# Stick-breaking attention taken by pairs of heads, sums and top-k steps paced, gates multiplied into the output weights of two half projections

## The chip, the cores and the metric

The kernel runs on one core of one Trainium2 chip. The core has TensorE (PE, with its weight loads listed as PEld), VectorE (DVE), ScalarE (ACT), GpSimd (POOL) and SyncE (SP, which only issues transfers). The metric is the device time of one execution in microseconds; lower is better.

## The reference

Two layers, each a mixer and a SwiGLU block, over 512 tokens of width 1024 in float32. Six vectors a layer, made from `c` by one product with `w_mod`, shift, scale and gate them. The change touches the first half of layer 0, the even mixer, and the output projection of layer 1's mixer.

```python
mod = einsum('bd,ldm->lbm', silu(c), w_mod) + b_mod       # per layer: sh_m, sc_m, g_m, sh_f, sc_f, g_f
h = x * (1 + sc_m) + sh_m
# layer 0: even mixer
z = q_sb @ k_sb.T * 64**-0.5                               # 8 heads, 512 x 512
log_keep = where(past, log_sigmoid(-z), 0)
suffix = reverse_cumsum(log_keep) - log_keep
o_sb = where(past, exp(log_sigmoid(z) + suffix), 0) @ v_sb
score = sum_h relu(q_ix @ k_ix.T * 64**-0.5)[h] * w_ix[h]  # 4 index heads; the best 128 keys of each row are kept
o_dsa = softmax(masked(rope(q_dsa) @ rope(k_dsa).T)) @ v_dsa   # 8 heads
y = concat(o_sb, o_dsa) @ w_out_even
# layer 1: differential attention, then y = o @ w_out_odd
x = layer_norm(ALPHA * x + (1 + g_m) * y)
x = layer_norm(ALPHA * x + (1 + g_f) * swiglu(x * (1 + sc_f) + sh_f))
```

## The kernel before

Everything is laid out by a Python program that issues instructions for tiles; a scheduler then puts them in a fixed order on each engine (earlier in the program comes first, but an instruction that is not ready lets later ones past), and allots tile buffers. Generators `yield` the PE time in microseconds that they have just issued, and `weave(main, fill, ratio)` runs `ratio` microseconds of `fill` for each microsecond that `main` yields.

Every float32 operand of a dense product is split into a high part (`wh`, `hh`, `o_h`, float32r, copied by ACT) and a low part (`wl`, `hl`, `o_l`, the difference); `mm3` (L319) makes three products of them and counts as 0.65. `split_w` (L292) splits 128x1024 of weights: ACT copies, and the engine at the head of the list `low` subtracts (`low_on`, L288, sets that list; in layer 0 it is VectorE).

Layer 0's mixer, in program order:
- `proj_tokens` (L987) makes `v_sb`, with `index_scores` (L755) and then `top_keys` (L779) stepped beside it. `top_keys` is 16 rounds of `max` and `match_replace` for each of three blocks of 512, 384 and 256 columns, all on VectorE, one `yield` a round.
- `sb_heads` (L816) is stick-breaking attention. For one head, `scores_of` makes 1280 columns of scores in three PSUM banks (of six in the tag `z`) from float32 operands of 64 rows, each followed by a 128-row product that adds the mask; ACT runs Abs, Exp and Ln, VectorE joins them (L834) and copies the high part `hi` (L835), POOL makes `lo` (L836). `suffix` adds the running sums as 20 products of 128 rows (L847) and ACT takes Exp. `mix` (L855) weighs the values for two heads, one in each half of the columns. Head h+2's scores are issued between the suffixes of two heads.
- `weave(..., rest, SB_FILL)` lays `even_rest` behind it: ten dense 128-column tiles of 24 products each, three pairs of q and k tiles for the later heads and four q tiles with rope for the next part. One step of `topk` goes with each dense step, and one step of `mods0` with each fourth dense step and with each yield of `sb_heads`.
- `mods0` is three calls of `mod_side` (L188). Each loads 16 pieces of `w_mod` (256 KB, tag `wm`, three buffers that also hold the sum `macc`) and adds them up on VectorE, one piece a step (L210, L212); call 2 ends in the gate row `rows[0, 2]` (`grow`), calls 3 and 4 in the shift and scale for the block behind.
- `dsa_heads` (L915) is the sparse attention, a pipeline of 16 units, with `down_beside` (L577) woven in: the first half of the output projection, 32 steps of `mm3`, each finished PSUM bank going through `partial` (L476), which multiplies by `grow` and adds to the residual `xa`. `mods0` is stepped with every second of them, and drained behind.
- `down_last` (L608) is the second half of the projection, followed by layer norm and the transposes `turn` for the SwiGLU block.

Layer 1 does the same with `diff_heads` and `down_beside(w_out_odd[0], ...)` (L1169).

Of the kernel before, what the change touches and what calls it, by code (L numbers as in the profile page):

```python
# [26 lines left out]
SB_FILL = 1.0  # L27
DSA_FILL = 0.65
# [19 lines left out]
def hybrid_kernel(ctx, tc, x, c, positions, w_mod, b_mod, w_in_even, w_out_even, w_in_odd,  # L48
# [139 lines left out]
    def mod_side(l, i, wide=False):  # L188
# [12 lines left out]
        for h in range(2):  # L201
# [12 lines left out]
            if wide:  # L214
                yield
# [260 lines left out]
    def partial(o, b, cs, grow, first):  # L476

        t = wd("yt")[:, :cs.stop - cs.start]
# [300 lines left out]
    def top_keys():  # L779

        for i in range(3, 0, -1):
            sc = scores[i]
            for r in range(16):
# [3 lines left out]
                yield  # L787
# [28 lines left out]
    def sb_heads(qk):  # L816
        Z, WT = {}, {}

        def scores_of(h):
            q, k = qk[h // 2]  # L820
            need(q, k)
            pb = 64 * (h % 2)
            z = Z[h] = [bank("za"), bank("zb"), bank("zc")]
            for s, (i, f, _, n) in enumerate(STRIP):
                pe.matmul(z[i][:, f:f + n], lhsT=k[pb:pb + 64, P * s:P * s + P], rhs=q[pb:pb + 64, P * s:S],
                          start=(f == 0), stop=False, skip_group_check=True)
                pe.matmul(z[i][:, f:f + P], lhsT=ident_r, rhs=bias_sb_r, start=False, stop=True, skip_group_check=True)
            hi, lo = ab("hi", F32R), ab("lo", F32R)
            for i, a, b in SPAN:
                zi, e, l = z[i][:, :b - a], slice(a, b), wd("l")[:, :b - a]  # L830
                act.activation(l, zi, AF.Abs)
                act.activation(l, l, AF.Exp, scale=-1.0)
                act.activation(l, l, AF.Ln, bias=1.0)
                dve.scalar_tensor_tensor(l, zi, 0.0, l, op0=OP.max, op1=OP.add)  # L834
                dve.tensor_copy(hi[:, e], l)  # L835
                pool.tensor_tensor(lo[:, e], l, hi[:, e], op=OP.subtract)  # L836
            WT[h] = hi, lo
            return 4.3 if h > 5 else 2.3

        def suffix(h):  # L840
            z, (hi, lo) = Z[h], WT[h]
            for s in (0, 1, 3, 2):
                i, f, _, n = STRIP[s]
                for s2 in range(s, 4):
                    _, _, c2, n2 = STRIP[s2]
                    for op in (hi, lo):
                        pe.matmul(z[i][:, f + n - n2:f + n], lhsT=negtri_r if s2 == s else negones_r,  # L847
                                  rhs=op[:, c2:c2 + n2], start=False, stop=True, skip_group_check=True)
            w = ab("w")
            for i, a, b in SPAN:  # L850
                act.activation(w[:, a:b], z[i][:, :b - a], AF.Exp)
            WT[h] = w
            return 2.1

        def mix(hp):  # L855
            o = Z[2 * hp + 1][0]
            for s, (_, _, c0, n) in enumerate(STRIP):
                for j in range(2):
                    h = 2 * hp + j
                    pe.matmul(o[64 * j:64 * j + 64, S - n:S], lhsT=v_sb[s][:, 64 * h:64 * h + 64], rhs=WT[h][:, c0:c0 + n],  # L860
                              start=(s == 0), stop=(s == 3), skip_group_check=True)
            put_o(hp, o)
            return 2.1

        yield scores_of(0)
# [416 lines left out]
```

## Time and profile before

| | |
|---|---|
| median of three runs | 1331.32 us (1330.69 to 1336.52) |
| profiled execution, its own time | 1333.38 us |
| its span, first to last instruction | 1331.3 us |
| mean granted TensorE clock | 0.985 of full speed |
| busy: PE, DVE, ACT, POOL | 96%, 67%, 37%, 19% of the span |

The shares are averages over stages with different limits. A busy PE is not a PE at its peak, since the ends of matmuls are modelled: at full rate, matmuls of 512 columns start 0.22 us apart and are each shown as 0.39 us long. So PE's work is counted here from start to start. Stick-breaking attention runs from 95 to 228 us of the span, the sparse attention from 228 to 298, the end of the projection and the layer norm to about 314.

### The profile page before, as it was taken

How to read it: one execution, taken by the hardware profiler on the slowest of the kernel's cores; microseconds unless marked ns; L12 is line 12 of the kernel's file. 1: busy time of each engine (PE TensorE's matmuls, PEld its weight loads, DVE VectorE, ACT ScalarE, POOL GpSimd, SP SyncE). 2: the span in 40 equal slices, each digit the busy share in tenths (PEclk: the TensorE clock that was granted, in tenths of full speed). 3: DMA queues.
4: the chain of work that ended last, by engine and by line, in shares of the span. 5: the costliest groups of instructions: out<-in, count | busy, mean ns of one | idle time of the engine just before them, and what ended most of it. 6: DMA issues, size and time to landing. Idle time of an engine off the chain costs nothing.

```text
span 1331.3 us, 17597 instructions
## 1 busy us (share of the span) xinstructions
PE 1283.0 (96%) x6707; PEld 1017.8 (76%) x6707; DVE 885.8 (67%) x1605; ACT 498.8 (37%) x889; POOL 246.4 (19%) x173
## 2 busy tenths in 40 slices
PE   6999998999999999999999999898999999999995
PEld 5767676668888888888888866676888888888884
DVE  3789996987866665665694387787786335335358
ACT  2445544554432222222244356565443322322210
POOL 0103223001800000000017244443280000000004
PEclk9999989999999999999999999999999999999998
DMA  9953234342365555555423422215235223233211
GB/s 265 279 174 95 88 112 139 99 126 96 92 219 157 192 169 173 190 172 189 141 68 111 127 64 84 88 52 175 78 97 190 75 100 110 95 96 95 95 64 63
DMA packets 134388, 169.47 MB, mean 127 GB/s; under 512 B 7800, under 2 KB 89120, under 8 KB 134304
## 3 DMA queue, kind: packets, MB, share of 16 engines
q1 hardware_dynamic: 133568, 167.31, 39.9%
q8 instruction: 52, 0.85, 0.3%
q10 hardware_dynamic: 576, 1.02, 0.2%
q14 instruction: 32, 0.26, 0.1%
q0 software_dynamic: 160, 0.03, 0.0%
HBM read 159.95 MB, written 2.10 MB: 122 GB/s over the span
## 4 chain that ended last, share of the span: by engine, by line
PE 49%; issue 26%; DVE 13%; ACT 4%; DMA 3%; POOL 3%; SPq 1%; DVEq 0%; ACTq 0%; POOLq 0%
PE po L321 7%; PE po L322 7%; PE po L323 7%; PE pd L321 4%; PE pd L323 4%; PE pd L322 4%; DMA wm<-in_w_mod_dram 2%; PE pv L321 1%; PE pv L322 1%; PE pv L323 1%; DMA rt<-rq 1%; PE pf L322 1%; PE pf L323 1%; PE pf L321 1%; DVE yt L479 1%
## 5 line engine op out<-in xcount | busy, mean ns | idle before, releaser
L295 ACT ACTIVATE wh<-raw 128x1024 fp32r<-128x1024 f32 x174 | 183.8, 1065 | 499.8 <-PE po L322 268.6
L299 DVE TENSOR_TENSOR wl<-raw,wh 128x1024 fp32r<-128x1024 f32 x169 | 238.3, 1414 | 169.5 <-ACT wh L295 169.3
L321 PE MATMUL po<-hh,wh 128*128 128x512 f32 x848 | 340.9, 402 | 0.4 <-DVE sg L631 0.3
L323 PE MATMUL po<-hh,wl 128*128 128x512 f32 x848 | 333.4, 393 | 0.0
L322 PE MATMUL po<-hl,wh 128*128 128x512 f32 x848 | 333.3, 393 | 0.0
L321 PEld LDWEIGHTS po<-hh,wh 128*128 128x128 f32 x848 | 160.6, 189 | 40.0 <-issue 6.4
L323 PEld LDWEIGHTS po<-hh,wl 128*128 128x128 f32 x848 | 160.8, 190 | 34.1
L322 PEld LDWEIGHTS po<-hl,wh 128*128 128x128 f32 x848 | 160.9, 190 | 30.4
L502 POOL TENSOR_TENSOR lnv<-lnv,mhalf 128x1 f32<-128x1 f32 x16 | 11.6, 723 | 683.7 <-DVE lnv L500 683.5
L322 PE MATMUL pd<-wl,hid_h 128*128 128x512 f32 x352 | 137.2, 390 | 0.0
L323 PE MATMUL pd<-wh,hid_l 128*128 128x512 f32 x352 | 137.0, 389 | 0.0
L321 PE MATMUL pd<-wh,hid_h 128*128 128x512 f32 x352 | 137.0, 390 | 0.0
L212 DVE SCALAR_TENSOR_TENSOR macc<-wm,silu_c,macc 128x512 f32<-128x512 f32 x140 | 108.1, 775 | 6.8 <-DMA wm<-in_w_mod_dram 4.6
L631 DVE TENSOR_TENSOR sg<-sg,po 128x512 f32<-128x512 f32 x40 | 27.5, 686 | 118.3 <-PE po L323 118.3
L321 PEld LDWEIGHTS pd<-wh,hid_h 128*128 128x128 f32 x352 | 66.1, 188 | 14.1 <-issue 0.4
L322 PEld LDWEIGHTS pd<-wl,hid_h 128*128 128x128 f32 x352 | 66.1, 188 | 13.8 <-DVE wl L299 0.3
L323 PEld LDWEIGHTS pd<-wh,hid_l 128*128 128x128 f32 x352 | 66.1, 188 | 13.7
L479 DVE TENSOR_TENSOR yt<-pd,grow 128x512 f32<-128x512 f32 x96 | 64.1, 682 | 10.2 <-PE pd L323 10.1
L321 PE MATMUL pd<-wh,o_h 128*128 128x512 f32 x128 | 57.0, 445 | 0.0
L323 PE MATMUL pd<-wh,o_l 128*128 128x512 f32 x128 | 51.8, 405 | 0.0
L322 PE MATMUL pd<-wl,o_h 128*128 128x512 f32 x128 | 51.4, 401 | 0.3 <-DVE wl L299 0.3
L1094 ACT ACTIVATE e<-e,nm 128x128 f32<-128x128 f32 (+3 forms) x64 | 35.4, 555 | 36.8 <-DVE nm L1093 25.2
(276 smaller groups left out, 2021.4 us busy)
## 6 DMA issues: line engine op xcount, KB each, us to landing
wm<-in_w_mod_dram SPq DMA_DIRECT2D x56, 512.0 KB, 5.0
raw<-in_w_gate_dram SPq DMA_DIRECT2D x22, 1024.0 KB, 5.4
raw<-in_w_up_dram SPq DMA_DIRECT2D x22, 1024.0 KB, 5.4
wm<-in_w_mod_dram SPq DMA_DIRECT2D x80, 256.0 KB, 4.0
raw<-in_w_down_dram SPq DMA_DIRECT2D x16, 1024.0 KB, 5.1
raw<-in_w_in_odd_dram SPq DMA_DIRECT2D x12, 1024.0 KB, 5.2
raw<-in_w_in_even_dram SPq DMA_DIRECT2D x6, 1024.0 KB, 7.7
raw<-in_w_down_dram SPq DMA_DIRECT2D x12, 512.0 KB, 3.3
```

The source lines that it names most:

```text
L212: dve.scalar_tensor_tensor(a, t[:, k, :], silu_c[:, k0 + k:k0 + k + 1], a, op0=OP.mult, op1=OP.add)
L295: act.activation(oh, src, AF.Copy)
L299: e.tensor_tensor(ol, src, oh, op=OP.subtract)
L321: pe.matmul(o, lhsT=ah, rhs=bh, start=start, stop=False, skip_group_check=True)
L322: pe.matmul(o, lhsT=ah, rhs=bl, start=False, stop=False, skip_group_check=True)
L323: pe.matmul(o, lhsT=al, rhs=bh, start=False, stop=stop, skip_group_check=True)
L479: dve.tensor_tensor(t, o, grow[:, cs], op=OP.mult)
L502: norm_done["pow"] = pool.tensor_tensor(y, v[:, 1:2], mhalf[:, 0:1], op=OP.pow).ins
L631: dve.tensor_tensor(g, g, o, op=OP.mult)
L1094: act.activation(es[j], es[j], AF.Exp, scale=-1.0, bias=nm, accum_out=ss[:, j, i:i + 1])
```

## The change

- `scores_of`, `suffix` and `mix` now take a pair of heads. Scores are issued strip by strip for both heads of a pair, which lie in rows 0 to 63 and 64 to 127, all score products of a batch first and the mask products behind them; there are two batches, banks 1 and 2 (`late`) and bank 0 (`first`). A pair holds all six banks. ACT now copies `hi` instead of VectorE.
- `SB_COST` gives what each stage yields, 51.7 in all over four pairs; no step of `mods0` goes with `sb_heads` itself any more.
- `sums` and `paced`: while dense tiles are issued, 1.4 us of VectorE work goes with each 1 us; a top-k round yields 0.27(i+1)+0.28, and one step of `mods0` goes with each third step of `topk`. `mod_side` yields once more for each half, which makes 18 steps a call.
- `low_on(pool)` stands around the weave: the low weight parts of `even_rest` are made on POOL.
- `gated_rows` loads half of the 4x128 output weight rows and multiplies them by the gate row on POOL (two instructions of 128x1024 a half), in both layers; `partial` then needs one VectorE instruction instead of two. The first half is loaded early where `ts` is given.

```diff
+SIDE = 1.4
+SB_COST = (6.5, 3.2, 2.4, 0.3, 0.6)
...
 def mod_side(l, i, wide=False):
...
-            if wide:
-                yield
+            yield
...
     def partial(o, b, cs, grow, first):
 
+        if grow is None:
+            t = xa[b][:, cs]
+            if first:
+                dve.scalar_tensor_tensor(t, t, ALPHA, o, op0=OP.mult, op1=OP.add)
+            else:
+                dve.tensor_tensor(t, t, o, op=OP.add)
+            return
...
-    def down_beside(w, k0, ops, grow, first):
-
+    def gated_rows(w, k0, h, gate):
+
+        t = rows_w(w, k0, 4, h)
+        for k in range(0, 4, 2):
+            v = t[:, k:k + 2, :]
+            pool.tensor_tensor(v, v, gate[:, HALF[h]].unsqueeze(1).to_broadcast([P, 2, S]), op=OP.mult)
+        return t
+
+    def down_beside(w, k0, ops, grow, first, ts=None):
+
+        first_t = ts.pop() if ts else gated_rows(w, k0, 0, grow)
         for h in range(2):
-            t = rows_w(w, k0, 4, h)
+            t = first_t if h == 0 else t1
             ws = split_k(t[:, 0:2, :]) + split_k(t[:, 2:4, :])
             for b in range(4):
                 bs = slice(P * b, P * b + P)
                 o = acc("pd")
+                if (h, b) == (0, 0):
+                    t1 = gated_rows(w, k0, 1, grow)
...
-                partial(o, b, HALF[h], grow, first)
+                partial(o, b, HALF[h], None, first)
...
+            if b == 1:
+                yield 0.1
...
-                yield
+                yield 0.27 * (i + 1) + 0.28
...
     def sb_heads(qk):
...
+        def scores_of(hp, banks):
+            q, k = qk[hp]
             need(q, k)
+            for i in banks:
+                for j in range(2):
+                    Z[hp, i, j] = bank("z" + "abc"[i])
+            strips = [(s, *STRIP[s]) for s in (1, 3, 2, 0) if STRIP[s][0] in banks]
+            for s, i, f, _, n in strips:
+                for j in range(2):
+                    own = slice(64 * j, 64 * j + 64)
+                    pe.matmul(Z[hp, i, j][:, f:f + n], lhsT=k[own, P * s:P * s + P], rhs=q[own, P * s:S],
+                              start=(f == 0), stop=False, skip_group_check=True)
+            for s, i, f, _, n in strips:
+                for j in range(2):
+                    pe.matmul(Z[hp, i, j][:, f:f + P], lhsT=ident_r, rhs=bias_sb_r, start=False, stop=True, skip_group_check=True)
+            for j in range(2):
+                if (hp, j) not in HL:
+                    HL[hp, j] = ab("hi", F32R), ab("lo", F32R)
+                hi, lo = HL[hp, j]
+                for i, a, b in SPAN:
+                    if i in banks:
...
-                dve.tensor_copy(hi[:, e], l)
+                        act.activation(hi[:, e], l, AF.Copy)
+                        pool.tensor_tensor(lo[:, e], l, hi[:, e], op=OP.subtract)
...
+        late, first = (1, 2), (0,)
+        scores_of(0, late)
+        scores_of(0, first)
+        yield SB_COST[0]
         for hp in range(4):
+            suffix(hp, late)
+            yield SB_COST[1]
+            suffix(hp, first)
+            yield SB_COST[2]
             if hp < 3:
+                scores_of(hp + 1, late)
+                yield SB_COST[3]
+            mix(hp)
+            yield SB_COST[4]
             if hp < 3:
+                scores_of(hp + 1, first)
+                yield SB_COST[0]
...
-    rest = beside(even_rest(), topk, 1)
...
-    rest = beside(rest, mods0, 4)
-    weave(beside(sb_heads(qk_sb), mods0, 1), rest, SB_FILL)
+    def sums():
+        for n, cost in enumerate(topk):
+            yield cost or 1.5
+            if n % 3 == 2:
+                next(mods0, None)
+                yield 0.85
+    def paced(main, side, rate):
+        owed = 0.0
+        for cost in main:
+            owed += cost * rate
+            while owed > 0:
+                got = next(side, None)
+                if got is None:
+                    break
+                owed -= got
+            yield cost
+    rest = paced(even_rest(), sums(), SIDE)
+    low_on(pool)
+    weave(sb_heads(qk_sb), rest, SB_FILL)
+    low_on(dve)
...
     def even_fill(rest):
-        yield from rest
+        ts = []
+        for n, cost in enumerate(rest):
+            if n >= 4 * KT and got_rows and not ts:
+                ts.append(gated_rows(w_out_even[0], 0, 0, rows[0, 2]))
+            yield cost
         while not got_rows:
             next(mods0)
-        yield from beside(down_beside(w_out_even[0], 0, oT[:4], rows[0, 2], True), mods0, 2)
+        yield from beside(down_beside(w_out_even[0], 0, oT[:4], rows[0, 2], True, ts), mods0, 2)
         drain(mods0)
...
     def odd_fill():
         yield from rest
+        ts = [gated_rows(w_out_odd[0], 0, 0, rows[1, 2])]
...
-        yield from down_beside(w_out_odd[0], 0, oT[:4], rows[1, 2], True)
+        yield from down_beside(w_out_odd[0], 0, oT[:4], rows[1, 2], True, ts)
```

## Rows read from the trace of the kernel before

**Rows 1.** Windows: busy us by engine (instructions), granted clock, DMA share, GB/s
```profile
95.00:228.00 133.00, 131.31 (x592) 90.96 (x590) 115.59 (x249) 71.56 (x138) 36.65 (x30) 0.95 0.36 109
228.00:234.00 6.00, 1.40 (x7) 0.95 (x8) 4.40 (x6) 1.34 (x2) 1.97 (x2) 0.90 0.14 44
234.00:298.00 64.00, 63.68 (x447) 43.32 (x447) 57.29 (x169) 35.95 (x96) 5.15 (x4) 0.96 0.35 107
380.00:400.00 20.00, 20.00 (x90) 16.57 (x89) 12.84 (x17) 6.00 (x9) 0.00 (x0) 1.00 0.56 183
860.00:928.00 68.00, 63.15 (x356) 48.07 (x355) 56.97 (x161) 38.49 (x90) 27.44 (x18) 1.00 0.35 113
```

**Rows 2.** Chain that ended last, 90 to 330 us: start, us, what
```profile
118.19 0.68 DVE score L786 x2
...
170.60 1.05 PE za L825 x2
...
220.02 6.57 DMA rt<-rq
...
231.97 0.60 DVE kd_l L924
```

**Rows 3.** Timeline of PE: start, us, what, count in a merged line
```profile
121.26 1.12 PE L825 MATMUL za<-q_sb,k_sb 64*128 64x512 f32 x2
122.31 0.33 PE L827 MATMUL za<-cst_r 128*128 128x128 f32 x1
122.57 0.91 PE L825 MATMUL zb<-q_sb,k_sb 64*128 64x384 f32 x2
...
125.13 0.44 PE L322 MATMUL po<-hl,wh 128*128 128x512 f32 x1
...
165.27 2.37 PE L860 MATMUL za<-w,v_sb 128*64 128x512 f32 x16
167.58 0.50 PE L321 MATMUL po<-hh,wh 128*128 128x512 f32 x1
...
217.76 0.39 PE L847 MATMUL za<-hi,cst_r 128*128 128x512 f32 x1
...
220.46 0.45 PE L321 MATMUL po<-hh,wh 128*128 128x512 f32 x1
```

**Rows 4.** Groups of VectorE and ScalarE, 95 to 314 us: count, busy us, mean ns
```profile
L835 DVE CAST hi<-l 128x512 fp32r<-128x512 f32 x16 | 7.0, 437 | 0.0
L835 DVE CAST hi<-l 128x256 fp32r<-128x256 f32 x8 | 2.8, 346 | 0.0
L299 DVE TENSOR_TENSOR wl<-raw,wh 128x1024 fp32r<-128x1024 f32 x15 | 18.9, 1264 | 0.3 <-ACT wh L295 0.3
L479 DVE TENSOR_TENSOR yt<-pd,grow 128x512 f32<-128x512 f32 x13 | 8.9, 681 | 2.0 <-PE pd L323 1.8
L212 DVE SCALAR_TENSOR_TENSOR macc<-wm,silu_c,macc 128x512 f32<-128x512 f32 x37 | 31.4, 849 | 4.6 <-DMA wm<-in_w_mod_dram 4.6
L805 ACT ACTIVATE o_h<-ot 128x512 fp32r<-128x512 f32 x7 | 4.4, 633 | 0.2
```

**Rows 5.** Groups of POOL over the whole span, with mean ns
```profile
L540 POOL TENSOR_TENSOR xa<-xa,lng 128x1024 f32<-128x1024 f32 x12 | 34.9, 2931 | 0.0
...
L299 POOL TENSOR_TENSOR wl<-raw,wh 128x1024 fp32r<-128x1024 f32 x5 | 12.1, 2423 | 7.2 <-ACT wh L295 4.0 <-issue 3.3
```

**Rows 6.** Timelines of POOL and VectorE around 213 us
```profile
212.86 2.43 POOL L836 TENSOR_TENSOR lo<-l,hi 128x512 fp32r<-128x512 f32 x2 [2.40 <-DVE hi L835]
...
213.13 1.57 DVE L212 SCALAR_TENSOR_TENSOR macc<-wm,silu_c,macc 128x512 f32<-128x512 f32 x1
```

**Rows 7.** Timeline of VectorE from 78 us
```profile
83.66 0.74 DVE L212 SCALAR_TENSOR_TENSOR macc<-wm,silu_c,macc 128x512 f32<-128x512 f32 x1
...
100.26 0.68 DVE L834 SCALAR_TENSOR_TENSOR l<-za,l 128x512 f32<-128x512 f32 x1
```

**Rows 8.** Loads of L196, 195 to 236 us
```profile
DMA to landing us min/median/max: 2.6/2.8/5.4
```

More of the change, by code (lines that the diff above doesn't have):

```diff
@@ L816, in sb_heads @@
     def sb_heads(qk):
-        Z, WT = {}, {}
-        def scores_of(h):
-            q, k = qk[h // 2]
+        Z, HL, W = {}, {}, {}
+        def scores_of(hp, banks):
+            q, k = qk[hp]
             need(q, k)
[L822 to L834, printed above, removed]
-                dve.tensor_copy(hi[:, e], l)
-                pool.tensor_tensor(lo[:, e], l, hi[:, e], op=OP.subtract)
-            WT[h] = hi, lo
-            return 4.3 if h > 5 else 2.3
@@ L840, in suffix @@
[L840 to L853, printed above, removed]
+            for i in banks:
+                for j in range(2):
+                    Z[hp, i, j] = bank("z" + "abc"[i])
@@ new lines, in scores_of @@
+            for j in range(2):
[4 more added lines that the diff above has]
+                    if i in banks:
+                        zi, e, l = Z[hp, i, j][:, :b - a], slice(a, b), wd("l")[:, :b - a]
+                        act.activation(l, zi, AF.Abs)
+                        act.activation(l, l, AF.Exp, scale=-1.0)
+                        act.activation(l, l, AF.Ln, bias=1.0)
+                        dve.scalar_tensor_tensor(l, zi, 0.0, l, op0=OP.max, op1=OP.add)
+                        act.activation(hi[:, e], l, AF.Copy)
+                        pool.tensor_tensor(lo[:, e], l, hi[:, e], op=OP.subtract)
@@ new lines, in weights_of, with suffix @@
+        def weights_of(hp, j, a, b):
+            part = a >= S
+            if (hp, j, part) not in W:
+                if j == 0:
+                    w = ab("w")
+                    W[hp, j, 0], W[hp, j, 1] = w[:, :S], w[:, S:]
+                elif part:
+                    W[hp, j, part] = T("row", [P, D], F32, 2, "w")
+                else:
+                    W[hp, j, part] = r1("w")
+            return W[hp, j, part][:, a - S * part:b - S * part]
+        def suffix(hp, banks):
+            for j in range(2):
+                hl = HL[hp, j]
+                for s in (0, 1, 3, 2):
+                    i, f, _, n = STRIP[s]
+                    if i not in banks:
+                        continue
+                    for s2 in range(s, 4):
+                        _, _, c2, n2 = STRIP[s2]
+                        for op in hl:
+                            pe.matmul(Z[hp, i, j][:, f + n - n2:f + n], lhsT=negtri_r if s2 == s else negones_r,
+                                      rhs=op[:, c2:c2 + n2], start=False, stop=True, skip_group_check=True)
+                for i, a, b in SPAN:
+                    if i in banks:
+                        act.activation(weights_of(hp, j, a, b), Z[hp, i, j][:, :b - a], AF.Exp)
@@ L859, in mix @@
                     h = 2 * hp + j
-                    pe.matmul(o[64 * j:64 * j + 64, S - n:S], lhsT=v_sb[s][:, 64 * h:64 * h + 64], rhs=WT[h][:, c0:c0 + n],
+                    pe.matmul(o[64 * j:64 * j + 64, S - n:S], lhsT=v_sb[s][:, 64 * h:64 * h + 64], rhs=weights_of(hp, j, c0, c0 + n),
                               start=(s == 0), stop=(s == 3), skip_group_check=True)
             put_o(hp, o)
-            return 2.1
-        yield scores_of(0)
-        yield scores_of(1)
+        late, first = (1, 2), (0,)
+        scores_of(0, late)
+        scores_of(0, first)
+        yield SB_COST[0]
         for hp in range(4):
-            yield suffix(2 * hp)
+            suffix(hp, late)
+            yield SB_COST[1]
+            suffix(hp, first)
+            yield SB_COST[2]
             if hp < 3:
-                yield scores_of(2 * hp + 2)
-            yield suffix(2 * hp + 1)
-            yield mix(hp)
+                scores_of(hp + 1, late)
+                yield SB_COST[3]
+            mix(hp)
+            yield SB_COST[4]
             if hp < 3:
-                yield scores_of(2 * hp + 3)
+                scores_of(hp + 1, first)
+                yield SB_COST[0]
     turned = [None]
```

2 lines of the change are left out of this document (1 added, 1 removed).

## Prediction

> **What bounds the kernel now.** I read the windows first, then the chain, then PE's own timeline. The windows cut the changed part of layer 0 into stick-breaking attention (133 us), a gap of 6 us, and sparse attention with the first half projection (64 us) [rows 1]. VectorE is busy for 115.6 of the 133 and 57.3 of the 64; PE's record is full in both, which says little. ScalarE has 71.6 of 133, POOL 36.7. The chain changes engine within the stage [rows 2]: around 118 us it runs along VectorE, where top-k rounds stand in front of the heads' own instructions; around 170 us along PE's score products; from about 195 us along rope's shuffles and the loads of `wm`, which share SP's queue (a shuffle is on it for 6.57 us at 220.02); and at 231.97 the sparse attention waits for VectorE to make `kd_l`. So no one engine bounds the stage.
>
> How much of the 133 us does PE need? A dense product takes 20.00/90 = 0.222 us [rows 1]; 10 tiles x 24 = 240 of them are 53.3. One head's scores run from 121.26 to 125.13, 3.87 us; eight are 31.0. A suffix is 220.46-217.76 = 2.70; eight are 21.6. A `mix` is 167.58-165.27 = 2.31; four are 9.2 [rows 3]. Together 115.1 us. The other 18 us are waits and half-speed clock (0.95 granted, so about a tenth of the stage lay at 1.2 GHz after slack stretches) [rows 1].
>
> **The change part by part.**
>
> *Scores by pairs.* Each head's 1280 columns become two PE records per product, and every mask product, 128 columns and so worth 0.06, takes 122.57-122.31 = 0.26 us to the next start [rows 3], since it stands between 64-row products; the turn costs 0.2. Batching leaves two turns a batch, four a pair. Do the two heads' records overlap, now that they lie in different row halves? No row of before has float32 records in two row halves. The nearest is `mix`: 16 float32 records in two column halves, of the same column counts as one pair's scores, in 2.31 us [rows 3]. The lower bound is that, plus 8 masks at 0.06 and four turns at 0.2: 3.6 a pair. The upper bound is no overlap: two heads' score products at 3.87-4 x 0.26 = 2.83, plus the same 1.3: 6.9. Now a pair costs 7.74. I take 3.9, near the `mix` row; PE needs 4 x 3.84 = 15.4 us less (3.2 to 16.6), 99.7 in all.
>
> The Trainium skill, "TensorE: Matmul & The Clock Gate", Part 3, says that matmuls start and end strictly in order, whatever their tile. Here each product's two records follow each other in the same half, so only every second could overlap, a pair's scores would take about 2.9 instead of 2.3, and the gain would be 13 instead of 15.4. The `mix` row has the same order and is faster, so I keep the row.
>
> *`hi` moves.* VectorE loses 16 x 0.437 + 8 x 0.346 = 9.8 us; ScalarE gains 16 x 0.633 [rows 4] and 8 of half the width, at no more than that each: 12.6 to 15.2, I take 13.5, and it stands at 71.6+13.5 = 85. The copy now stands in each head's chain on the engine that also does Abs, Exp and Ln.
>
> *Low parts on POOL.* Ten instructions of 1.264 leave VectorE (12.6) [rows 4], and cost POOL 10 x 2.42 = 24.2 [rows 5]: 61 in the stage. A `lo` may queue 2.4 us behind one.
>
> *Sums paced.* Before, 20 yields of `sb_heads` and a quarter of 80 dense steps step `mods0` 40 times in this stage; now topk's remaining 50 steps give 16. By program order 24 x 0.849 = 20.4 us of VectorE work [rows 4] leave for the sparse attention. But the order is not strict: the first sum ran at 83.66, before the first head's VectorE work at 100.26, though the program has it later [rows 7]. VectorE's load in the stage becomes 115.6-9.8-12.6 = 93, or 73 with those sums gone.
>
> *The stage.* All engines now lie below PE's 99.7: ScalarE 85, VectorE 73 to 93, POOL 61. A pair holds all six banks, so the next pair's scores start only after this pair's late Exps. What hides the chain is 13 us of dense work a pair (6.5+3.2+2.4+0.3+0.6) beside some 12 of its own PE work; ScalarE has 85/4 = 21 us a pair. If that cover held wholly the stage would take 100; with the 18 us of waits as they are, 118. I take 8 us of waits, since top-k no longer stands in the chain's way but four engines are each near four fifths: 108, so -25 (-15 to -33).
>
> *The gap.* At 228 to 234 the thinner sums free SP and VectorE, but the gate row is new in the path: its 19th step is reached only when the sparse attention begins (16 were taken), and then POOL needs 2 x 2.93 [rows 5] before the first split. For the same reason the early load through `ts` never happens in layer 0: `got_rows` is empty until `rest` is used up. 0 (-5 to +5).
>
> *The sparse attention.* VectorE: 57.3 + 20.4 - 8 x 0.681 = 72.3 against 64 [rows 1, 4]. If the scheduler brings no sum forward, that is 8 us more; if all, none. Four gate products put 4 x 2.93 = 11.7 on POOL; beside POOL a sum took 1.57 instead of its mean 0.849 [rows 4, 6], so each may cost VectorE between nothing and 2.93; I take 1. And when the gate row is made, 36 steps of `mods0` are left; the 32 dense steps take 16, so the whole fourth call, 16 sums, comes behind them in a lump. Together +6 (0 to +20).
>
> *Layer 1.* VectorE loses another 8 x 0.681 = 5.4 of 57 us in 68 [rows 1, 4], POOL gains 11.7 on 27.4, with slack on both: -1 (-4 to +4).
>
> **Sum.** -25+0+6-1 = -20. The profiled execution took 1333.4 us, which becomes 1313.4; it lies 2.1 above the median, so the forecast for the median is **1311 us**. The ends of the terms add up to -42 and +14.
>
> **The rivals.**
> - *More of the waits go*, and the sums run in VectorE's idle time: stage at 100, nothing given back: -33-1 and a gap closed by up to 5: 1292 to 1301. For it: [rows 7] and the loads below PE's. Against: four engines near full rarely mesh.
> - *POOL is the new drag.* In the stage, `lo` behind ten low parts of 2.42 delays each suffix; in both attentions, gate products hold VectorE for their whole length, 11.7 us each: 1311 + 11.7 and up to half of it again in layer 1, 1321 to 1331. For it: the 1.57 in [rows 6]. Against: that row lost 0.72, not POOL's whole 1.2. The Trainium skill's page "SBUF — State Buffer", "SBUF: two separate sides", has such a lock: a VectorE instruction with two SBUF inputs and a GpSimd one exclude each other for the whole instruction; by it this rival would be the forecast, and the row bears out about half of it.
> - *The sums' tail, the case on the slow side.* `mods0` is drained behind the last dense step, and the shift and scale it makes are needed by the first transposes behind the layer norm. With three `wm` buffers, one the sum, two loads are in flight, so a step takes (2.8+0.849)/2 = 1.8 us [rows 4, 8]; 16 steps are 29 us. VectorE's partials and norms come behind them. If nothing brings them forward and nothing hides them: 1331-25+29-1 = 1334; with the stage's gain at 20 or less, 1339 and more (1327 to 1346). It decides when more than 14 sums, 25/1.8, are left behind the last dense step. Against it is [rows 7].
> - *The change doesn't do what it says* holds for the early gate load in layer 0 only (above); the forecast has it.
>
> **How the numbers follow.** Chances: forecast's case (1301 to 1321) 0.50; more 0.15; POOL 0.20; tail 0.15. A measurement can tell about 0.5%, 6.7 us, from no change (the three runs spread over 0.44%). Faster by that, under 1324.7: 0.50+0.15+half of POOL's 0.10 = 0.75. Within it, to 1338: the other 0.10 and 0.06 of the tail = 0.16. Slower: the tail's 0.09. The range leaves out half of the case of more (below 1296) and 0.12, most of the tail, above 1333: 1296 to 1333.
>
> **What would show it.** In the profile after: the first sparse `zq` product near 203 instead of 228; a pair's 16 score records within 3 us; at most 0.6 us between a batch's masks; `hi` in ScalarE's groups; PE waiting for `lo` before a suffix by no more than 2 us a pair. Sums between the last dense `pd` of the first half and the transposes would show the tail. Long VectorE sums or divisions beside the gate products would show POOL. I am wrong if a pair takes over 30 us (the cover fails), or if the stretch from the first `zq` to the transposes grows from 86 us by over 14.

## The result and the profile after

The changed kernel takes **1370.0 us** (median of 6 runs, 1366.8 to 1374.3) against 1333.3 us for the kernel before on the same chips: a ratio of **1.0281, interval 1.026 to 1.0303**. It is slower by 37 us. The forecast was 1311 us with a range of 1296 to 1333, so the result lies outside of it, on the side that had 0.09 of the chance. The profiled execution has a span of 1368.4 us against 1331.3, 37.1 more.

Where the 37 us lie is read from four landmarks on PE: the first score product of the heads, the first `zq` of the sparse attention, the first `tx` (the layer norm's transposes) and their end.

| stretch | before, us | after, us | difference |
|---|---|---|---|
| up to the first score product | 95.7 | 98.2 | +2.5 |
| stick-breaking stage, to the first sparse `zq` | 132.2 | 142.9 | +10.7 |
| first `zq` to first `tx` | 85.4 | 105.3 | +19.9 |
| the transposes `tx`, first to last | 19.6 | 23.3 | +3.7 |
| all that follows, layer 1 with it | 998.4 | 998.7 | +0.3 |

The windows of the kernel after, with the columns of [rows 1], cut the same stretches; the third is the end of the sparse attention, and the last is dense work.

```profile
98.00:241.00 143.00, 121.46 (x576) 87.89 (x573) 100.90 (x205) 78.59 (x159) 62.13 (x40) 0.89 0.25 81
241.00:302.00 61.00, 60.50 (x412) 40.96 (x411) 55.37 (x160) 35.46 (x93) 11.08 (x6) 0.92 0.31 102
302.00:331.00 29.00, 10.28 (x70) 7.52 (x65) 12.68 (x21) 2.41 (x7) 0.00 (x0) 0.73 0.60 199
```

Compare with [rows 1]: the stage has VectorE at 100.9 where it had 115.6. That is 14.7 less, where `hi` and the low parts alone were to take off 22.4 and the sums up to 20 more. PE's record is no longer full (121.5 of 143), and the clock is 0.89 instead of 0.95. In the third window every engine is idle for more than half of the time.

Names in the lines that follow: `w` are the exponentials that `mix` weighs with, `ot` is ScalarE's copy of a finished `mix`, `rq` a q or k tile on its way through rope, `ix` an index score of top-k. `macc` is a sum of `mods0`, `pm` the PE product that adds such a sum up over its rows, `mh` and `ml` the high and low part of it for the gate row. `e` are the weights of the sparse attention, `tp` and `pt` their transposes.

*The pairs do what they should.* The timeline of PE shows the third pair's late batch, the second pair's `mix` and the third pair's first batch:

```profile
162.55 1.14 PE L851 MATMUL zb<-q_sb,k_sb 64*128 64x384 f32 x8
163.52 0.60 PE L851 MATMUL zc<-q_sb,k_sb 64*128 64x256 f32 x4
164.05 0.66 PE L855 MATMUL zb<-cst_r 128*128 128x128 f32 x4
...
165.61 2.37 PE L904 MATMUL za<-w,v_sb 128*64 128x512 f32 x16
167.92 1.12 PE L851 MATMUL za<-q_sb,k_sb 64*128 64x512 f32 x2
168.97 0.33 PE L855 MATMUL za<-cst_r 128*128 128x128 f32 x1
...
176.85 2.07 PE L851 MATMUL za<-q_sb,k_sb 64*128 64x512 f32 x2 [5.66 <-ACT ot L825]
```

Twelve score records, three of the four products of both heads, take 164.05-162.55 = 1.50 us, so the two heads overlap: the four products of one head alone took 2.83 before, without their masks [rows 3]. But in front of the second head's part of the first batch PE stands still for 5.66 us. Its bank is held by the `mix` output until ScalarE has copied `ot`. Why `ot` is late is on the other two engines (idle time before, and what ended it, in brackets):

```profile
167.59 0.39 ACT L863 ACTIVATE l<-zc 128x256 f32<-128x256 f32 x1
173.73 0.94 ACT L867 ACTIVATE hi<-l 128x512 fp32r<-128x512 f32 x2 [5.75 <-DVE l L866]
174.57 0.92 ACT L864 ACTIVATE l<-l 128x512 f32<-128x512 f32 x2
175.40 0.92 ACT L865 ACTIVATE l<-l 128x512 f32<-128x512 f32 x2
176.22 0.57 ACT L825 ACTIVATE ot<-za 128x512 f32<-128x512 f32 x1
```

```profile
172.69 0.41 DVE L807 MATCH_REPLACE8 score<-top,score 128x256 f32<-128x256 f32 x1
173.01 0.68 DVE L866 SCALAR_TENSOR_TENSOR l<-zb,l 128x512 f32<-128x512 f32 x1
```

`ot` is queued on ScalarE behind the next pair's `hi`, which waits for VectorE's max-and-add, which stands behind 15 top-k rounds in a row (their `match_replace` starts from 158.92 to 172.69). The waits of PE in the stage, summed (us in total, times, longest):

```profile
PE za L851 <- ACT ot L825: 14.2, 3, 6.5
PE zb L893 <- POOL lo L868: 2.9, 4, 0.9
PE ix L793 <- ACT w L897: 2.2, 1, 2.2
PE pm L223 <- ACT mh L221: 2.0, 1, 2.0
```

The kernel before has one line of this kind in its whole stage (95 to 228 us):

```profile
PE pm L223 <- DVE ml L221: 1.5, 2, 1.0
```

*The sums' tail.* The chain from 302 us is a load of `wm` and a sum in turn, and PE stands behind it:

```profile
302.31 4.76 DMA wm<-in_w_mod_dram
...
307.16 0.76 DVE macc L214
307.94 6.32 DMA wm<-in_w_mod_dram
...
314.35 0.76 DVE macc L214
...
319.23 2.69 DMA wm<-in_w_mod_dram
...
322.01 0.76 DVE macc L214
322.79 2.64 DMA wm<-in_w_mod_dram
...
329.94 0.66 PE pm L232 x8
```

```profile
PE pm L232 <- DVE macc L214: 18.6, 2, 14.4
```

From 307.16 us on, VectorE has eleven sums left. The last dense `pd` work and the last `o_dsa` are still to be done then; they stand in PE's queue behind `pm`. The two long loads share the DMA engines with loads for the work behind (`lng` and `lnb`, issued at 301.88 and 302.78, and 1 MB of `raw` at 306.28): their share is 0.94 from 307.0 to 314.5 us, and 0.38 from there to 330.

### The profile page after: what moved, and what is told of

Same layout as the page of the kernel before. It is cut to its first block, busy times and chain, and to the rows that moved or that the text cites. A ratio compares the mean times of both kernels' runs of the same rounds, so it can differ in the third digit from the quotient of the medians.

```text
span 1368.4 us, 17587 instructions
## 1 busy us (share of the span) xinstructions
PE 1282.7 (94%) x6707; PEld 1019.8 (75%) x6707; DVE 875.7 (64%) x1555; ACT 507.6 (37%) x913; POOL 290.4 (21%) x191
## 4 chain that ended last, share of the span: by engine, by line
PE 48%; issue 25%; DVE 12%; DMA 5%; ACT 4%; POOL 3%; SPq 2%; DVEq 0%; ACTq 0%; POOLq 0%
PE po L322 7%; PE po L323 7%; PE po L324 7%; PE pd L322 5%; PE pd L324 4%; PE pd L323 4%; DMA wm<-in_w_mod_dram 3%; DVE score L807 2%; PE zq L938 1%; DVE top L806 1%; PE pf L323 1%; PE pf L324 1%; PE pf L322 1%; PE pv L323 1%; PE pv L324 1%
## 5 line engine op out<-in xcount | busy, mean ns | idle before, releaser
L300 DVE TENSOR_TENSOR wl<-raw,wh 128x1024 fp32r<-128x1024 f32 x159 | 224.9, 1418 | 166.4 <-ACT wh L296 166.1
L323 PEld LDWEIGHTS po<-hl,wh 128*128 128x128 f32 x848 | 161.9, 191 | 30.9
L323 PEld LDWEIGHTS pd<-wl,hid_h 128*128 128x128 f32 x352 | 66.1, 188 | 13.8 <-DVE wl L300 0.2
L487 DVE TENSOR_TENSOR yt<-pd,grow 128x512 f32<-128x512 f32 x80 | 52.9, 680 | 8.8 <-PE pd L324 8.8
```

Source lines behind the costliest of these rows:

```text
L300: e.tensor_tensor(ol, src, oh, op=OP.subtract)
L323: pe.matmul(o, lhsT=ah, rhs=bl, start=False, stop=False, skip_group_check=True)
L487: dve.tensor_tensor(t, o, grow[:, cs], op=OP.mult)
```

## The experiments

The stage is from the first score product to the first sparse `zq`; its gaps are PE's idle times of over 0.4 us in it; the sparse stretch runs on to the first `tx`. All three are of each kernel's profiled execution, one for each kernel; the ratio is to the kernel before, measured beside it.

| kernel | median us | ratio, interval | stage | gaps | sparse stretch |
|---|---|---|---|---|---|
| before | 1333.3 | | 132.2 | 1.5 | 85.4 |
| after | 1370.0 | 1.0281, 1.026 to 1.0303 | 142.9 | 21.4 | 105.3 |
| sums sooner | 1338.7 | 1.0036, 1.0016 to 1.0056 | 147.5 | 22.4 | 77.5 |
| mix sooner | 1364.5 | 1.0230, 1.0191 to 1.0269 | 137.2 | 16.9 | 108.8 |
| both | 1339.9 | 1.0043, 1.0021 to 1.0065 | 144.2 | 18.8 | 78.2 |
| plain down | 1366.2 | 1.0241, 1.0199 to 1.0283 | 141.0 | 19.2 | 103.7 |
| pairs alone | 1330.2 | 0.9978, 0.9953 to 1.0003 | 133.1 | 11.8 | 80.0 |
| heads again | 1347.7 | 1.0123, 1.0075 to 1.017 | 139.5 | 4.9 | 86.3 |
| both, hi on VectorE | 1341.2 | 1.0072, 1.0044 to 1.01 | 145.8 | 24.2 | 79.9 |
| both, low parts on VectorE | 1329.4 | 0.9964, 0.9941 to 0.9987 | 137.5 | 16.3 | 76.5 |
| pairs, mix | 1331.7 | 0.9999, 0.9979 to 1.0019 | 133.9 | 11.7 | 80.5 |
| no new work on POOL | 1339.1 | 1.0040, 1.0023 to 1.0057 | 133.6 | 15.9 | 84.4 |
| paced alone | 1353.7 | 1.0156, 1.0126 to 1.0187 | 127.0 | 0.0 | 106.1 |
| gates alone | 1337.8 | 1.0035, 1.0016 to 1.0055 | 135.5 | 6.5 | 81.7 |
| low parts alone | 1339.8 | 1.0044, 1.0023 to 1.0064 | 138.0 | 8.9 | 84.0 |
| few rounds | 1325.2 | 0.9934, 0.9913 to 0.9956 | 134.0 | 13.8 | 76.2 |
| pairs, gates | 1333.3 | 0.9993, 0.9972 to 1.0014 | 139.8 | 19.6 | 73.7 |
| sums later | 1361.0 | 1.0201, 1.0155 to 1.0248 | 143.9 | 23.6 | 94.3 |
| even sums | 1329.8 | 0.9976, 0.9959 to 0.9993 | 135.1 | 17.9 | 78.0 |
| no loads | 1327.0 | 0.9950, 0.9929 to 0.9971 | 133.6 | 12.8 | 74.7 |

What stands ahead of the first score product takes 93.8 to 100.0 us in these profiles. It differs even between kernels whose programs are the same up to there: 98.2 us in after, 99.1 in sums later, 96.3 in plain down, 95.5 in mix sooner. So 3 us between two kernels need not come from what was edited.

### Where the sums stand

**Sums sooner**, on the kernel after:

```
             if n % 3 == 2:
                 next(mods0, None)
+                next(mods0, None)
                 yield 0.85
```

> Two steps of `mods0` instead of one after each third top-k step: 36 of its 54 steps are taken in the stick-breaking stage instead of 18, and none is left behind the 32 dense steps of the first half projection. If the loss lies in the sums' tail (PE stood still for some 20 us between 310.6 and 330.5), 18 to 24 us go: about 1349 us, with the stretch from the first sparse score product to the layer norm's transposes back near 86 us. If VectorE is what the stage lacks, the 18 further sums (15 us) lengthen the stage by as much, and the time stays at 1365 to 1372.

31 us go, more than expected. The stage is longer by 4.6 us, with 31 sums in it instead of 18, and the tail is gone, which the window shows at the place of the idle 29 us:

```profile
303.00:319.00 16.00, 16.00 (x72) 13.15 (x71) 12.65 (x25) 3.83 (x7) 0.95 (x1) 1.00 0.23 72
```

**Sums later**, on the kernel after: the sums in the sparse attention instead.

```
-        yield from beside(down_beside(w_out_even[0], 0, oT[:4], rows[0, 2], True, ts), mods0, 2)
+        yield from beside(down_beside(w_out_even[0], 0, oT[:4], rows[0, 2], True, ts), mods0, 1)
```

> The kernel after with a step of mods0 after each of the 32 dense steps of the first half projection instead of after each second: 4 of the 54 steps are left behind them instead of 20. If the tail is only a matter of where the sums stand, 20 to 28 us go: 1342 to 1350. If VectorE is full in the sparse attention (54 of 64 us), the 16 further sums (12 us) push the softmax back, and 10 to 15 us go: 1355 to 1360. If the loads of wm are what is late, the tail only moves: 1364 or more.

9 us go, a little less than the middle case: the stretch is 94.3 us, between the two. A wait of 4.3 us remains at `pm`, and in between PE's `tp` waits for VectorE's `e` (1.8 us) and `pt` (0.8).

**Paced alone**: `sums()`, `paced()` and the costed yields of `top_keys` on the kernel before; heads one by one, low parts and gates as they were.

> The kernel before with nothing but the pacing of top-k and sums (one sum after every third top-k step): heads one by one, low parts and gates as before. If the tail of sums is the change's main loss and belongs to the pacing alone, this kernel has it: 18 to 31 us over before, 1352 to 1365, with sums between the last dense pd and the transposes. If the tail needs the shorter stage or POOL's work too, it stays within 8 us of before.

The tail belongs to the pacing. Its windows (stage, sparse attention, tail) and the one wait of PE:

```profile
99.00:226.00 127.00, 127.00 (x572) 88.98 (x569) 109.89 (x234) 70.06 (x134) 38.98 (x30) 0.96 0.28 86
226.00:301.00 75.00, 66.88 (x462) 46.12 (x461) 64.41 (x180) 37.01 (x97) 6.64 (x6) 0.99 0.41 134
301.00:330.00 29.00, 13.66 (x76) 10.35 (x77) 16.24 (x31) 5.25 (x11) 0.00 (x0) 0.67 0.25 74
```

```profile
PE pm L232 <- DVE macc L214: 20.1, 2, 14.6
```

The stage itself is the shortest of all kernels, 127.0 us and no gap: the pacing is worth 5 us there, and costs 21 in the sparse stretch.

### The pairs

**Mix sooner**, on the kernel after, and **both** with sums sooner:

```
             suffix(hp, first)
             yield SB_COST[2]
+            mix(hp)
+            yield SB_COST[4]
             if hp < 3:
                 scores_of(hp + 1, late)
                 yield SB_COST[3]
-            mix(hp)
-            yield SB_COST[4]
-            if hp < 3:
                 scores_of(hp + 1, first)
```

> A pair's `mix` stands ahead of the next pair's late scores, so that ScalarE copies `ot` out of the bank before the next pair's Abs, Exp, Ln and `hi`. If the bank that `ot` holds is what stops PE in front of the next first batch (2.7, 6.3 and 6.9 us), 10 to 16 us go: 1354 to 1360. If the length of a pair's own chain sets the stage, the waits only move to the suffix: 1366 to 1372.

> Both edits. If the two losses are separate places of the path, the gains add up: 28 to 40 us less, 1330 to 1342, about the kernel before. If VectorE or ScalarE as a whole sets the stage, the sum is less than the larger of the two alone allows: 1350 or more.

The wait for `ot` goes and the stage falls by 5.7 us, but 3.5 of them come back in the sparse stretch; a further 2.7 us of the difference lie ahead of the stage, where the edit changes nothing. The 1364.5 us lie between the two cases, nearer to the second, and the waits moved as that one had it: in both, PE waits 8.5 us for `mh` in front of `pm` and 6.7 us for `lo` and `hi`. The 1339.9 us of both lie in the range of its first case, but the gains do not add up: it is no better than sums sooner alone.

**Pairs alone** is the kernel before with the new `sb_heads`; **pairs, mix** has the edit above too; **heads again** is sums sooner with the old `sb_heads`.

> The kernel before with nothing but the new pairs of heads (score products of both heads in turn, masks together, hi copied by ScalarE, late and first batches with their own yields); top-k, sums, low parts and gates as before. If PE's score work is what the stage lacks, the 13 to 15 us that the scores save appear: 1318 to 1324. If a pair's six held banks make the chain (ScalarE, VectorE, POOL in turn) the limit, the gain is eaten by waits before the suffixes and the first batches: 1330 to 1350, with over 10 us of gaps on PE in the stage where the kernel before has 1.5.

> The kernel before with the pairs of heads and mix ahead of the next pair's late scores, nothing else of the change. The pairs alone measured 1330.2 against 1333.2, with PE stopped 3.9 and 1.4 us in front of first batches at the bank that ot holds. If that bank is what still eats the scores' gain, 3 to 6 us more go: 1324 to 1327. If a pair's chain is the limit, the wait moves to the suffix: 1329 to 1332.

> The kernel after with two sums a step, but the heads one by one as in the kernel before (hi on VectorE too); pacing, low parts on POOL and gated rows stay. If the pairs cost time against the heads, it is faster than the 1338.7 of the same kernel with pairs: 1320 to 1330. If low parts on POOL and the pacing make the waits, they stay here too, and PE has 15 us more to do: 1340 to 1355.

The pairs gain little against the heads: 3 us alone, which is not clear of no change (0.9953 to 1.0003), and 9 us beside the rest of the change. What they gain is not in the stage, which is longer with pairs: 133.1 us for 132.2 alone, 147.5 for 139.5 beside the rest. There the scores' saving is eaten by the gaps. Most of the gaps belong to the pairs: heads again has the pacing and the low parts on POOL too, and 4.9 us of gaps for 22.4. So its time falls in the second case, but not for that case's reason. The gain stands in the sparse stretch, 80.0 us for 85.4 and 77.5 for 86.3: in front of the first `zq` PE waits 4.6 us for VectorE (`kd_l`, `qd_l`) in before and 6.3 in heads again, and 0.3 and 1.7 with pairs. Why VectorE is earlier there was not tried. (The profile of heads again is of the fastest of its four runs, 1340.7 us.)

Moving `mix` in pairs alone gave nothing: its wait for `ot` (5.3 us) became a wait for `hi` (3.5 us at 172.6) and one for `pm`. By kinds of PE's work in the stage, in us (from one record's start to the next's, gaps apart; index scores and `pm`, 3 to 5 us, are left out):

```
                 scores  masks  dense  suffix   mix   gaps  stage
before             23.4    7.5   63.5    22.7  10.3    1.5  132.2
after              15.2    4.5   64.5    24.5   9.2   21.4  142.9
pairs alone        14.2    4.3   66.6    23.3   9.2   11.8  133.1
mix sooner         10.1    4.4   60.5    31.7   9.2   16.9  137.2
few rounds         10.1    4.4   64.2    27.2   9.2   13.8  134.0
no loads           10.1    4.4   64.0    28.0   9.2   12.8  133.6
```

**Few rounds** and **no loads** are both with low parts on VectorE; their expectations say what they leave out.

```
+                if r == 0:
+                    top = T("top8", [P, 8], F32, 2)
+                    dve.max(out=top, in_=sc)
+                    dve.match_replace(out=sc, in_to_replace=top, in_values=sc, imm_value=TAKEN)
```
```
-                    ahead.append(load(*todo.pop(0), n))
+                    p = todo.pop(0)
+                    if wide or p == (0, 0):
+                        one = load(*p, n)
+                    ahead.append(one)
```

> The kernel with pairs, mix sooner, sums sooner and low parts on VectorE (1329.4), with one top-k round of sixteen in each of the three row blocks: 45 of 48 rounds are left out, so the sparse attention attends to fewer keys; all yields and the order of the rest stay. If the chains wait behind top-k on VectorE, the gaps in front of suffixes, pm and index (about 15 us) and the half clock after them go, and the stage falls from 137 to about 115 us: 1303 to 1312. If a chain through ScalarE, VectorE and POOL is too long by itself, the gaps stay at 10 us or more: 1320 to 1328.

> The kernel with pairs, mix sooner, sums sooner and low parts on VectorE (1329.4), but of the 16 loads of wm per modulation vector in layer 0 only the first is made, and all 16 sums read that tile: 45 loads are left out, and the modulation that follows is another. If sums that wait for loads block VectorE's queue in front of the chains, the 10.5 us of such waits go, and pm's gaps of 3.3, 4.7 and 2.2 us on PE with them: 1315 to 1321. If the chain is too long by itself, the stage stays within 4 us of 137 and the time at 1325 to 1330.

My theory that the chains wait behind top-k fell; both times lie in the second case. In few rounds VectorE is busy for half of the middle window, and the gaps hardly move; its queue now stands at sums whose load has not landed. The window, VectorE's wait and PE's waits of few rounds:

```profile
135.00:195.00 60.00, 51.68 (x258) 40.20 (x257) 30.66 (x33) 36.41 (x73) 25.43 (x17) 0.91 0.27 86
```

```profile
DVE macc L214 <- DMA wm<-in_w_mod_dram: 42.8, 20, 5.2
```

```profile
PE pm L223 <- ACT mh L221: 7.3, 2, 5.6
PE ix L793 <- ACT w L898: 3.2, 1, 3.2
PE pm L232 <- ACT rq L460: 2.4, 1, 2.4
```

In no loads that wait of VectorE is gone, it is busy for 55.9 of the same 60 us, and PE's waits are still these:

```profile
PE pm L226 <- ACT mh L224: 7.4, 2, 4.1
PE ix L796 <- ACT w L900: 3.5, 1, 3.5
PE pm L235 <- ACT rq L463: 1.1, 1, 1.1
```

Each takes away one thing that stands in front of a chain, and gives 2 to 4 us; the other takes its place. The longest wait in both lies in PE's own order: `pm` stands in front of a suffix, and its operand `mh` is queued on ScalarE behind the whole chain of the pair. In few rounds the `lo` of that suffix were made by 175.46 us, and PE stood still for `pm` until 178.44. This is read from the trace; no run moved `pm`.

**Even sums**, on the kernel after with mix sooner and low parts on VectorE, takes the sums one by one (`if n % 3:` with one step and `yield 0.425`).

> Pairs, mix sooner, low parts on VectorE, gated rows, and the sums one by one: one step of mods0 after two of three top-k steps instead of two together after each third (the same number, 36 or so). In the kernel with two together (1329.4) VectorE stood 10.5 us in the stage at sums whose load had not landed, against 5.9 in the kernel before. If these waits hold the chains, half of them go and the time with them: 1322 to 1327. If chains are late for other reasons: 1328 to 1332.

No difference from two together (1329.8 and 1329.4): the second theory.

### POOL and ScalarE

**Both, low parts on VectorE** drops `low_on(pool)`; **low parts alone** adds it to the kernel before; **both, hi on VectorE** has `dve.tensor_copy(hi[:, e], l)`.

> The kernel with sums sooner and mix sooner (1339.9), and the weights' low parts in the stage back on VectorE (ten of 1.26 us). If POOL's 2.4 us low parts hold back the heads' lo, 5 us or more go: 1335 or less. If VectorE's queue is what holds the chains, 12 us more on it lengthen them: 1343 to 1352.

> The kernel before with nothing but the weights' low parts of the stick-breaking stage on POOL. If POOL's 2.4 us low parts cost 10 us by themselves (beside POOL VectorE's own instructions run longer, and lo, rope's shuffles and low parts share POOL's queue): 1340 to 1346. If they cost only in the pairs' tighter chain: 1329 to 1336.

> The kernel with sums sooner and mix sooner (1339.9), and hi copied by VectorE. In the trace of that kernel ScalarE waits 6.2 us for VectorE's max-and-add behind top-k rounds and then has hi and the other head's three functions in one queue. If ScalarE's queue is what a chain waits for, 4 to 8 us go: 1332 to 1336. If VectorE's queue is, hi joins it, behind further top-k rounds and sums, and 10 us of work come back there: 1342 to 1352.

The low parts on POOL cost 10.5 us with pairs and, by the ratio, 5.9 without; of the 9.9 us by which the profile of low parts alone is longer than that of before, 3.8 lie ahead of the stage and 5.8 in it. VectorE got nothing for the move: its busy time over the span is the same with ten instructions more. First the page's line of both, then of both with low parts on VectorE:

```profile
PE 1268.2 (95%) x6707; PEld 1014.7 (76%) x6707; DVE 878.1 (66%) x1555; ACT 507.5 (38%) x913; POOL 289.9 (22%) x191
```

```profile
PE 1265.9 (95%) x6707; PEld 1014.7 (76%) x6707; DVE 876.6 (66%) x1565; ACT 507.1 (38%) x913; POOL 264.4 (20%) x181
```

The groups of VectorE say which instructions grew (60 to 340 us, the max 90 to 245 us; count, busy us, mean ns); first both, then with the low parts on VectorE:

```profile
L464 DVE TENSOR_TENSOR rt<-rt,sin_t 128x512 f32<-128x512 f32 x6 | 6.2, 1030 | 7.6 <-DMA rt<-rq 7.6
L796 DVE SCALAR_TENSOR_TENSOR score<-ixr,wix,score 128x512 f32<-128x512 f32 x4 | 4.7, 1186 | 1.2 <-ACT ixr L795 1.1
L789 DVE COPY score<-bias_c 128x128 f32<-128x128 f32 x3 | 2.6, 875 | 0.0
L806 DVE MAX8 top<-score 128x8 f32<-128x512 f32 x16 | 11.0, 685 | 0.1
```

```profile
L464 DVE TENSOR_TENSOR rt<-rt,sin_t 128x512 f32<-128x512 f32 x6 | 4.1, 687 | 4.8 <-DMA rt<-rq 4.8
L796 DVE SCALAR_TENSOR_TENSOR score<-ixr,wix,score 128x512 f32<-128x512 f32 x4 | 3.0, 750 | 0.9 <-ACT ixr L795 0.7
L789 DVE COPY score<-bias_c 128x128 f32<-128x128 f32 x3 | 0.5, 180 | 0.0
L806 DVE MAX8 top<-score 128x8 f32<-128x512 f32 x16 | 11.0, 687 | 0.2
```

These two, which read two tiles, grew by half or more in the mean; the max, which reads one, did not. The Trainium skill, "SBUF — State Buffer", "SBUF: two separate sides", has a VectorE instruction with two SBUF inputs and a GpSimd one shut each other out; these rows agree with it. Two inputs are not the whole of it: a copy, which reads one tile, grew most, and the sums, which read two, by 6% (943 for 888 ns). `hi` on either engine is the same within 4 us; the 1341.2 us fall in neither case.

**Plain down** gives layer 0's first half projection its gate back on VectorE, on the kernel after; **no new work on POOL** does so in both layers, with low parts on VectorE too, on both; **gates alone** puts the gated rows on the kernel before, **pairs, gates** on pairs alone.

> Layer 0's first half projection multiplies by the gate in the partials on VectorE again, as the kernel before does; four gate products of 2.9 us leave POOL, eight multiplications of 0.68 us come back to VectorE. If POOL's gate products hold up VectorE or the splits, 10 us or more go: 1360 or less. If the loss lies elsewhere, the time stays within 4 us of 1370.

> Pairs, mix sooner, sums sooner, low parts on VectorE, and both layers' gates back on VectorE: everything that the change newly gives POOL is gone. Low parts alone gave back 10 us (1339.9 to 1329.4). If the gate products hold up VectorE likewise (eight of 2.9 us), 4 to 8 us more go: 1322 to 1326. If they lie under other work, 1328 to 1331, or up to 1334 for the 16 multiplications of 0.68 us that come back to VectorE.

> The kernel before with nothing but the gated rows on POOL in both first half projections. By the forecast's steps the gate products lie under other work and VectorE is relieved by 5.4 us a layer: 1328 to 1334. If each of the eight products holds VectorE for its whole length of 2.9 us, up to 23 us more: 1340 to 1356.

> The kernel before with pairs and gated rows, nothing else. Pairs alone measured 1330.2; with gates alone the stretch from the first sparse product to the layer norm's transposes was 3.7 us shorter, though the whole was 1337.8. If the gates' gain stands where VectorE is full, 1325 to 1329; if gates cost 4 us a kernel as in the run of them alone, 1333 to 1337.

Plain down stays within 4 us of the kernel after: the loss lies elsewhere. The gated rows shorten the sparse stretch wherever no tail hides it: by 3.7 us on before, 6.3 on pairs, 7.9 on both with low parts on VectorE, and there the transposes behind it by a further 3.8 (20.0 for 23.8). That is why no new work on POOL came out slower, against both of my cases. But they lengthen the stage, by 3.3, 6.7 and 3.9 us: they are issued within it (at 160 and 190 us), and stand at the head of POOL's queue, in front of `lo` and rope's `rq`, until VectorE lets them go. By the program they wait for the gate row; the releasers that the view names are top-k instructions of the same queue. POOL's waits in the stage of pairs, gates:

```profile
POOL raw L590 <- DVE score L805: 11.5, 1, 11.5
POOL raw L590 <- DVE top L804: 7.9, 1, 7.9
```

Gates alone measured 0.35% over before, 4.7 us, between its two cases, but from the first score product to the end its profile and that of before agree (1235.8 and 1235.6 us). The difference of the two profiles stands ahead of that, where PE ran at half clock (1.2 GHz) for most of the stretch; the window of gates alone, then that of before:

```profile
84.00:96.00 12.00, 11.54 (x24) 5.58 (x24) 7.79 (x12) 3.73 (x7) 0.00 (x0) 0.57 0.35 110
```

```profile
84.00:96.00 12.00, 11.43 (x43) 6.25 (x41) 11.16 (x20) 7.36 (x14) 0.00 (x0) 1.00 0.41 133
```

The kernel after has 0.60 there, beside its +2.5 us. It does not follow the gates: pairs, gates has 1.00, and low parts alone, without gates, 0.57. What sets that clock was not tried, so the 4.7 us are not shown to be a cost of the gates.

## Why the prediction was wrong

The forecast was a sum of -20; the profiles give +37. The step that failed most is **the stage**, "I take 8 us of waits, since top-k no longer stands in the chain's way": -25 was forecast, +10.7 came, which is 36 of the 57 us of error. The second is **the sparse attention**, "+6 (0 to +20)": +19.9, and +3.7 in the transposes behind it.

- *The 18 us of waits*: wrong. They were a remainder, and there was little to win in it: PE waits for 1.5 us in the whole stage of before. Of the rest, 10.2 us are the 240 dense products, which took 63.5 us, 0.265 each, where the prediction has 53.3 at the full rate of [rows 1]; 3.3 are index scores and `pm`, which it has not at all. The same terms come back in the kernel after: of the 35 us between its stage and the 108 that were forecast, 13.4 are gaps (21.4 for 8), 11.2 dense products (the stage's clock is 0.89), 4.1 scores, 2.9 suffixes and 3.6 the work left out.
- *Scores by pairs*: right. Without the wait for `ot` (mix sooner), four pairs take 10.1+4.4 = 14.5 us, 3.6 a pair for 3.9 forecast, against 30.9 before: 16.4 saved for 15.4. In the kernel after it is 19.7, so 11.2 saved. Taken alone the records are 2.5 us a pair, between the 2.3 of the `mix` row and the 2.9 by strict order.
- *The cover*: wrong. The prediction counted cover as time and saw no order in it. But a pair ties three queues together: PE's first batch behind `ot`, `ot` behind the next chain on ScalarE, that chain behind whatever VectorE has in front (top-k here, sums that wait for loads where top-k is gone). A pair took 142.9/4 = 35.7 us, over the 30 that the prediction named as its refutation; the other one, a sparse stretch longer by over 14 us, came too. Gaps rose by 19.9 us, from 1.5 to 21.4, which is more than the 11.2 that scores and masks gave.
- *Top-k out of the way*: wrong. Paced by dense steps, it still came in runs of 15 rounds. But few rounds shows that it was not the limit by itself: 45 of 48 rounds less gave 4 us.
- *Low parts*: wrong in sign. -12.6 on VectorE was credited; VectorE's busy time did not fall, and the move costs 6 to 10 us. The rival "POOL is the new drag" had the mechanism in part: it hung VectorE's loss on the gate products, and on the low parts only the waits for `lo`, which are 2.9 us in the kernel after.
- *Gates*: +1 each forecast; they gain 4 to 8 us in the sparse stretch. They were not bound to the start of the sparse attention either: the first ran at 190.87 in the kernel after. They cost in the stage, through POOL's queue: in sum, with low parts on VectorE and sums sooner, the kernel is 10 us faster with them (1329.4 for 1339.1); alone and on pairs it is not faster.
- *The gap*: 0 forecast. The 4.4 us for which the first `zq` waits for `kd_l` in before are gone in the kernel after; the tail hides it in the sum.
- *Sums*: the rival "the sums' tail" came true, by its own mechanism: 1.8 us a sum was its price, and two sums every 3.5 us is what the chain shows. Its count was too high: eleven sums stood in the lump and not 16, since 24 had run before the sparse attention and not 16. But two of their loads took 4.8 and 6.3 us for 2.8, so PE still waits 18.6 us. Between the sparse stretches of after and sums sooner it is 28 us (105.3-77.5). Two things were missed: the prediction put a 0.15 chance on it on the strength of [rows 7], one sum that ran early, though pacing alone leaves the same tail; and it had the tail behind the last `pd`, while `pm` stands in front of the last ones in PE's queue, so that they wait too.
- *`hi`*: ScalarE's busy time grew by 8.8 us (498.8 to 507.6) for 13.5 forecast; the time is the same within 4 us with `hi` on either engine.
- *Layer 1*: -1 forecast, +0.3 measured for all behind the transposes.
- *More of the waits go*, the rival on the fast side, fell with the stage.

By single parts on the kernel before: pairs -3, gates +5, low parts +6, pacing +21: 29 of the 37 us. The pairs' part is not clear of no change, and the gates' part lies ahead of the stage. Nor do the parts simply add up: beside pairs the low parts cost 10.5 and not 6. Where the other 8 us come from is not shown.

Open: why the pairs keep 12 to 24 us of gaps in every form tried. Top-k and loads were taken away only one at a time; `pm` behind the suffix, which is the longest wait left, was not tried. The best versions, both with low parts on VectorE (0.9964) and even sums (0.9976), are ahead of the kernel before by under 0.5%: no form tried holds a gain of the size that was forecast.

## What to carry to other kernels

Before taking the remainder of a sum for waits, ask the profile for the waits: here 18 us of remainder held 1.5. Work that is thinned out in one stage must be followed to the place where its result is needed: count the steps left there, price each at its load's latency, and look at what stands behind the consumer in PE's queue. A saving on one engine is worth only what its neighbours' queues let through: for each instruction on the chain, name what is queued ahead of it on its own engine, and do not take dense time as cover. Before moving elementwise work to POOL, compare VectorE's mean durations beside POOL's; the busy time that moves may come back in them.

## What was not expected of the hardware

Score records of two heads in alternating row halves overlap almost wholly: 2.5 us for a pair, where one head's four products took 3.87-4 x 0.26 = 2.83 before [rows 3]. Ten low parts of 1.26 us taken off VectorE left its busy time where it was (878.1 and 876.6), since others ran longer: one index step that reads two tiles took 1186 ns in the mean for 750, and a copy 875 for 180. And loads of 256 KB that took 2.7 us at a DMA share of 0.38 took 4.8 and 6.3 beside other loads, at 0.88 and 0.94.
